# RWKV-7 chunk products of one core as 64x64 tiles on the four quadrants of TensorE, both scan directions side by side

## The chip, the cores and the metric

The kernel runs on one core of one Trainium2 chip. The metric is device microseconds from start to end of one execution, the median of the runs shown. TensorE (PE) does the matrix products, VectorE (DVE), ScalarE (ACT) and GpSimd (POOL) the element-wise work, and SyncE (SP) issues the DMAs.

## What is computed

Two layers of a bidirectional encoder (width 1024) on 2048 and 512 tokens. Layer 0 joins two gated linear recurrences. Layer 1 joins banded-window attention and RWKV-7 time mixing; the change is in the latter. Per head (8 heads of 64) and per direction it is this recurrence, and the two directions are added:

```python
def rwkv7_scan(r, log_w, k, v, kk, a):
    """S_t = S_{t-1} (diag(w_t) - kk_t (kk_t*a_t)^T) + v_t k_t^T, o_t = S_t r_t."""
    ...
    def step(S, inp):
        r_t, w_t, k_t, v_t, kk_t, b_t = inp
        s_kk = jnp.einsum('bhvk,bhk->bhv', S, kk_t)
        S = S * w_t[:, :, None, :] - s_kk[..., None] * b_t[:, :, None, :] + v_t[..., None] * k_t[:, :, None, :]
        return S, jnp.einsum('bhvk,bhk->bhv', S, r_t)
```

## The kernel before

Five stages follow each other: layer 0 with its input projection, its output projection, `layer1_proj` (projection of layer 1 and the element-wise preparation of the RWKV rows), `layer1_core` (attention and the RWKV recurrence) and the output projection of layer 1. All matrix products of `layer1_core` but the attention scores are plain float32; each such product is two records on TensorE (two weight loads, two passes), a transposition is one.

`layer1_core` works in 20 steps: 4 pairs of heads `p` times 5 blocks of 512 tokens. A step has two directions `d`, each two halves `hf` of four chunks `c` of 64 tokens. The two heads of a pair lie on partitions 0 to 63 and 64 to 127. Work is written as generators in lanes that take turns, and a planner of the framework then orders each engine's instructions at build time, by a simulated timeline and by priorities: `chain` first (1000), then `inverse` (600), then `stageT` (300), then `stageA` and attention.

- `stageA(n)` (lines 1279 to 1345) loads the prepared rows and makes, for each direction and half: `gram` (per head, 4 products 128x128x128 with a `KR` tile in which the other head's half is zero), its copy `GS`, masks into `LA`, `LD`, `OF`, `GB`, four transpositions `bk`, eight products `rps`, copied to `R`. PSUM: `pg`, two buffers of one bank.
- `inverse(n)` (lines 1347 to 1365): the 16x16 diagonal blocks of both directions go through DRAM (`lm`), are inverted by 28 small DVE operations and return through DRAM (`tm`).
- `stageT(n, d)` (lines 1367 to 1437), one lane per direction: reads `TC`, builds the 64x64 inverse in `TL` by 32x32 products `px`, `py`, `px`, `py`, then for each half `t1` (4 products), copies to `SW`, `fin` (2 times 4 products), sums into `RX`, copy to `OH`. PSUM: `pT`, two buffers of one bank.
- `chain(n, d)` (lines 1446 to 1492), one lane per direction, is the recurrence: per chunk a product `S0 x RX` (both heads at once), two DVE sums into `SS`, a transposition of `SS` on TensorE, an ACT copy scaled by the chunk's decay `ecol` to the next `S0`.
- `attention` (line 1561 on) runs beside: one block of 512 tokens of one group of heads for every two steps; per tile of 128 queries 4 score products, 12 transpositions `pt`, 3 products `po`. PSUM: `pa`, two buffers.

`stageA` of a step may be written at most NS = 4 halves ahead of `stageT`, since `GB`, `R` and `SW` have four buffers.

Of the kernel before, what the change touches and what calls it, by code (L numbers as in the profile page):

```python
# [40 lines left out]
class Common:  # L41
    def __init__(self, ctx, tc, a, seqs):
# [10 lines left out]
        self.lanes = {}  # L53
        nc.scalar.preload_act_table_set("natural_log_exp_and_others")
# [34 lines left out]
    def psums(self, ctx, l):  # L89
        f = lambda n, b: ctx.enter_context(self.tc.tile_pool(name=n + l, bufs=b, space=PSUM, reuse_waits="tile"))  # L90
        self.pp, self.pt, self.po = f("pp", 3), f("pt", 3), f("po", 2)

# [13 lines left out]
    def psum(self, n=NB):  # L106
        return self.pt.tile([128, n], F32, tag="t", name="pt")
# [711 lines left out]
def odd_cols():  # L819
# [7 lines left out]
    sw = list(range(64, 128)) + list(range(0, 64))  # L827
    for p in range(4):
        for off, perm in ((0, None), (512, None), (1024, sw), (1632, sw)):
            o = base + off + 128 * p  # L830
            out += [o + j for j in (perm or range(128))]
# [12 lines left out]
class Odd(Even):  # L844
# [47 lines left out]
    def rwkv_consts(self):  # L892
# [20 lines left out]
        self.xsc = self.const.tile([128, 2], F32, name="xsc")  # L913
        nc.vector.memset(self.xsc, 1.0)
        nc.vector.memset(self.xsc[0:64, 0:1], -0.5)
        nc.vector.memset(self.xsc[64:128, 1:2], -0.5)

        halves = slice(0, 64), slice(64, 128)
        self.bones = self.const.tile([128, 128], F32R, name="bones")
        self.swones = self.const.tile([128, 128], F32R, name="swones")  # L920
        for i in range(2):
            for j in range(2):
                q = halves[i], halves[j]
                self.act(self.bones[q], self.ident[q], AF.Copy, bias=float(i == j), scale=0.0)
                self.act(self.swones[q], self.ident[q], AF.Copy, bias=float(i != j), scale=0.0)
# [4 lines left out]
        self.v_scr = self.dram.tile([4, 2, nb, 64, 8, 128], F32, name="v_scr")  # L930
# [166 lines left out]
    def rwkv_rows(self, p, b, z):  # L1097
        nc, a = self.nc, self.a
        c64 = lambda t: t.rearrange("p (c t) -> p c t", t=RC)
        H0, H1 = slice(0, 64), slice(64, 128)  # L1100
# [68 lines left out]
        self.mm2(ps, self.swones, t)  # L1169
# [15 lines left out]
    def rwkv_dirs(self, p, b, kk, r, v, X1, X2, G):  # L1185
# [3 lines left out]
        for d in range(2):  # L1189
# [16 lines left out]
            self.stt(Z[:, 1, :, 0:64], view(X1), self.xsc[:, 0:1], e2, ALU.mult, ALU.mult)  # L1206
            self.stt(Z[:, 1, :, 64:128], view(X2), self.xsc[:, 1:2], e2, ALU.mult, ALU.mult)
# [13 lines left out]
    def layer1_core(self):  # L1221
        tc, nc, a = self.tc, self.nc, self.a
        with ExitStack() as ctx:
# [5 lines left out]
            pg, pT, pc = mkp("pg", 2), mkp("pT", 2), mkp("pc", 1)  # L1229
            pr = pg  # L1230
            self.pa = mkp("pa", 2)
            self.pt = pr
            mk = cp.tile([128, 2, 64], F32, name="mk")
            nc.sync.dma_start(out=mk, in_=a["mk"])
            mS = mk[:, 0:1].to_broadcast([128, 4, 64])
            mI = mk[:, 1:2].to_broadcast([128, 4, 64])
# [3 lines left out]
            M0, M1, MO = (mb[:, i:i + 1].to_broadcast([128, 8, 16]) for i in range(3))  # L1240
            ME = [mb[:, 3:4, i:i + 1].to_broadcast([128, 8, 16]) for i in range(2)]
# [10 lines left out]
            TL = [zeroed(f"TL{d}", [128, 8, 128], nc.vector) for d in range(2)]  # L1252
            SS = [[zeroed(f"SS{d}{i}", [128, 128], nc.vector) for i in range(2)] for d in range(2)]
            SW = [[[cp.tile([128, 4, 128], F32, name=f"SW{d}{i}{h}") for h in range(2)] for i in range(NS)] for d in range(2)]
            for i in range(NS):
                for d in range(2):
                    for h in range(2):
                        (nc.vector, nc.gpsimd)[h].memset(SW[d][i][h][Q[1 - h], :, Q[h]], 0.0)

# [500 lines left out]
```

## Time and profile before

| | us |
|---|---|
| median of 3 runs | 4167.64 (4167.12 to 4181.9) |
| the profiled execution | 4167.95 |
| its span, first to last instruction | 4166.2 |
| mean granted TensorE clock | 0.942 |

Over the span PE is busy 90%, DVE 68%, ACT 52%, POOL 27%. A busy PE is not a full PE: a record counts as busy until its result has left the array, so what the array really does is read from the distance between the starts of neighbouring records. `layer1_core` runs from about 2644 to 3808 us.

### The profile page before, as it was taken

The numbers are of one execution on the slowest core, as the hardware profiler recorded it, in microseconds if no ns is written. First come the engines' busy times: TensorE is split into PE (matmuls) and PEld (weight loads), VectorE is DVE, ScalarE is ACT, GpSimd is POOL, SyncE is SP. The second block draws the span as 40 slices with busy tenths as digits, with TensorE's granted clock in tenths as the row PEclk, the third lists the DMA queues.
The fourth block names the chain that finished last, engine by engine and source line by source line (L and its number), as shares of the span: only waits on it lengthen the run. The fifth ranks groups of instructions, "written<-read, shape, count | busy, mean of one in ns | idle before, by whom it ended". The sixth has DMA issues, their size and how long they took to land. (4 is left out here: it accounts for less than half of the span.)

```text
span 4166.2 us, 75101 instructions
## 1 busy us (share of the span) xinstructions
PE 3743.6 (90%) x27864; PEld 3067.3 (74%) x27864; DVE 2838.6 (68%) x6393; ACT 2149.8 (52%) x4198; POOL 1145.3 (27%) x1403
## 2 busy tenths in 40 slices
PE   6999999999888699999999989799999999995688
PEld 4878787777666577777777768578888888874567
DVE  4554545456666669757675768778777778775898
ACT  4565656555455432245454545556566666664220
POOL 1021212112211244423333322312222211113784
PEclk8999999999999799999999999899999999996889
DMA  7644445456555388768778876744454444534665
GB/s 264 215 144 165 167 148 202 155 193 217 210 207 198 109 251 253 232 230 263 242 258 260 252 250 218 197 103 117 109 121 116 118 119 118 125 79 150 222 223 173
DMA packets 768781, 770.20 MB, mean 185 GB/s; under 512 B 341632, under 2 KB 635136, under 8 KB 742816
## 3 DMA queue, kind: packets, MB, share of 16 engines
q1 hardware_dynamic: 768416, 765.40, 57.9%
q8 instruction: 221, 3.62, 0.4%
q14 instruction: 144, 1.18, 0.1%
HBM read 535.55 MB, written 220.20 MB: 181 GB/s over the span
## 5 line engine op out<-in xcount | busy, mean ns | idle before, releaser
L126 PE MATMUL pp<-h,whi 128*128 128x512 f32 (+2 forms) x4800 | 1565.7, 405 | 82.0 <-DMA h<-h_scr 29.0
L126 PEld LDWEIGHTS pp<-h,whi 128*128 128x128 f32 (+2 forms) x4800 | 895.4, 191 | 294.3 <-DMA h<-h_scr 30.5
L126 PE MATMUL pp<-h,wlo 128*128 128x512 f32 (+2 forms) x2400 | 958.5, 400 | 4.8 <-POOL wlo L113 4.7
L126 PEld LDWEIGHTS pp<-h,wlo 128*128 128x128 f32 (+2 forms) x2400 | 456.0, 190 | 110.5 <-POOL wlo L113 7.3
L110 ACT ACT_TABLE_LOAD x227 | 291.2, 1283 | 23.1 <-DVE cl L500 10.4
L126 PE MATMUL pp<-owh,oh 128*128 128x512 f32 x640 | 259.8, 406 | 23.6 <-DMA oh<-o_scr 22.6
L126 PE MATMUL pp<-owh,ol 128*128 128x512 f32 x640 | 256.2, 402 | 9.8 <-DMA ol<-o_scr 9.8
L1319 POOL COPY LD<-GS 32x128 f32<-32x128 f32 x320 | 115.1, 360 | 524.0 <-ACT GS L1316 508.7
L126 PE MATMUL pp<-owl,oh 128*128 128x512 f32 x640 | 259.1, 405 | 0.0
L113 POOL TENSOR_TENSOR wlo<-wst,whi 128x512 fp32r<-128x512 f32 (+3 forms) x87 | 161.0, 1856 | 248.4 <-ACT whi L110 244.8
L113 POOL TENSOR_TENSOR at<-abuf,abuf 64x256 f32<-64x256 f32 x80 | 63.7, 796 | 517.9 <-DVE abuf L530 448.3
L126 PE MATMUL gram<-KR,Zc 128*128 128x128 f32 x1280 | 188.5, 287 | 5.5 <-DMA KR<-z_scr 2.5
L126 PE MATMUL fin<-GB,SW 128*128 128x128 f32 x1280 | 179.4, 282 | 11.0 <-ACT OH L1433 8.1
L113 POOL TENSOR_TENSOR tmp<-tmp 128x512 fp32r<-128x512 f32 x80 | 116.6, 1457 | 256.6 <-ACT tmp L110 209.4
L113 DVE TENSOR_TENSOR SS<-chain,OH 64x64 f32<-64x64 f32 x608 | 135.1, 222 | 70.8 <-PE chain L126 59.5
L126 PEld LDWEIGHTS gram<-KR,Zc 128*128 128x128 f32 x1280 | 170.6, 201 | 8.6 <-ACT R L1334 3.1
L126 PEld LDWEIGHTS fin<-GB,SW 128*128 128x128 f32 x1280 | 161.2, 195 | 16.4 <-ACT OH L1433 11.4
L113 POOL TENSOR_TENSOR ptmp<-ptmp 128x512 f32<-128x512 f32 (+1 forms) x100 | 141.8, 1430 | 82.5 <-ACT ptmp L110 26.5
L126 PEld LDWEIGHTS pp<-owh,oh 128*128 128x128 f32 x640 | 125.5, 196 | 52.6 <-DMA oh<-o_scr 21.7
L110 ACT ACTIVATE S<-chain,ecol 128x128 f32<-128x128 f32 x320 | 115.4, 367 | 89.4 <-PE chain L141 86.0
L126 PEld LDWEIGHTS pp<-owh,ol 128*128 128x128 f32 x640 | 124.7, 195 | 37.7 <-DMA ol<-o_scr 11.7
L126 PE MATMUL chain<-RX,S 128*128 128x128 f32 x608 | 134.6, 310 | 14.0 <-DVE od L113 7.8
(327 smaller groups left out, 8330.5 us busy)
## 6 DMA issues: line engine op xcount, KB each, us to landing
h<-h_scr SPq DMA_DIRECT2D x70, 2048.0 KB, 9.2
h<-h_scr SPq DMA_DIRECT2D x80, 1024.0 KB, 7.4
z_scr<-Z SPq DMA_DIRECT2D x40, 1024.0 KB, 4.8
h_scr<-h SPq DMA_DIRECT2D x10, 2048.0 KB, 7.6
oh<-o_scr SPq DMA_DIRECT2D x40, 512.0 KB, 5.6
ol<-o_scr SPq DMA_DIRECT2D x40, 512.0 KB, 6.6
h_scr<-h1s SPq DMA_DIRECT2D x20, 1024.0 KB, 5.4
Zc<-z_scr SPq DMA_DIRECT2D x80, 256.0 KB, 3.2
```

The costliest lines, as they stand in the source:

```text
L110: self.nc.scalar.activation(out=out, in_=in_, func=func, bias=bias, scale=scale)
L113: (eng or self.nc.vector).tensor_tensor(out=out, in0=a, in1=b, op=op)
L126: self.nc.tensor.matmul(out=out, lhsT=lhsT, rhs=rhs, start=start, stop=stop)
L1319: nc.gpsimd.tensor_copy(LD[blk, cs], gs[blk, :, 32 * i:32 * i + 32])
```

## The change

In `layer1_proj` the two heads keep one order, so that three pairs of half-height DVE operations per block become three full ones, and `v_scr` is written by four DMAs per block and direction, not two. The columns and vectors that were swapped for this are no longer swapped.

In `layer1_core` the padding with zeros goes. Every chunk product becomes a 64x64 tile of the array: for direction 0 head h is read on its half and written on the same half, for direction 1 on the other half, so that the list `quads` names the four quadrants, and both directions share one tile (direction d in bank d of a PSUM tile of two banks). `stageA` and `stageT` run once per step for both directions; `pg` and `pT` become one buffer of two banks. `gram` becomes `gramb` and `gramk`; `bk` becomes products with diag(`ecol`) (made by POOL), so that `RX` carries the decay; `rps` becomes `kt` and `av`; `fin` becomes `finx` and `fino`, the latter with four 64-column products per chunk and quadrant. `t1` is read and written on the same half, so on two of the four quadrants. `chain` then needs per chunk two state products (one per head), one DVE sum and two output products: no transposition, no ACT copy. DMA loads per step fall from 32 to 12. `stageT` has one lane and single buffers (`TC`, `TE`, `TT`, `XS`, `T1`). In attention the lane yields after all four scores, and after every second transposed head.

The diff, cut to its core (what is removed stands in the code above):

```diff
@@ rwkv_rows @@
-        self.tt(X2[H0], k[H0], t[H0], ALU.mult)
-        self.tt(X1[H1], k[H1], t[H1], ALU.mult)
+        self.tt(X2, k, t, ALU.mult)
...
-        for h, x in ((H0, X2), (H1, X1)):
-            self.stt(t[h], r[h], self.rv[h, 5, p:p + 1], x[h], ALU.mult, ALU.mult)
-        self.stt(X1[H0], av[H0], 1.0, kk[H0], ALU.add, ALU.mult)
-        self.stt(X2[H1], av[H1], 1.0, kk[H1], ALU.add, ALU.mult)
+        self.stt(t, r, self.rv[:, 5, p:p + 1], X2, ALU.mult, ALU.mult)
+        self.stt(X1, av, 1.0, kk, ALU.add, ALU.mult)
@@ rwkv_dirs @@
-                nc.sync.dma_start(out=self.v_scr[p, d, db, :, o::2], in_=v4[64 * o:64 * o + 64])
+                for h in range(2):
+                    g = 64 * (h ^ d)
+                    nc.sync.dma_start(out=self.v_scr[p, d, db, g:g + 64, o::2],
+                                      in_=v4[64 * o:64 * o + 64, :, 64 * h:64 * h + 64])
@@ layer1_core @@
-            pg, pT, pc = mkp("pg", 2), mkp("pT", 2), mkp("pc", 1)
+            pg, pT, pc = mkp("pg", 1), mkp("pT", 1), mkp("pc", 1)
...
+            quads = [(d, Q[h], Q[h ^ d]) for d in range(2) for h in range(2)]
@@ stageA (new body of the loop over hf) @@
+                    kr = lp.tile([128, 2, 4, 192], F32, tag="KR", bufs=NS, name="KR")
+                    GB = lp.tile([128, 2, 4, 320], F32, tag="GB", bufs=4, name="GB")
...
+                    for d in range(2):
+                        nc.sync.dma_start(out=Z[:, d], in_=self.z_scr[p, d, b, :, 1, cs])
+                        nc.sync.dma_start(out=kr[:, d, :, 0:128], in_=self.z_scr[p, d, b, :, 0, cs])
+                        nc.sync.dma_start(out=vs[:, d], in_=self.v_scr[p, d, b, :, cs])
+                    gc = 8 * b + 4 * hf
+                    self.tt(kr[:, :, :, 128:192], iib,
+                            self.ecol[:, p, :, gc:gc + 4].unsqueeze(3).to_broadcast([128, 2, 4, 64]), ALU.mult, nc.gpsimd)
+                    two = lambda name: pg.tile([128, 2, 4, 128], F32, tag="t", name=name)
+                    gb = two("gramb")
+                    for c in range(4):
+                        for d, q, o in quads:
+                            self.mm(gb[o, d, c], Z[q, d, c, 0:64], kr[q, d, c, 0:128])
+                    gs = lp.tile([128, 2, 4, 64], F32, tag="GS", bufs=2, name="GS")
+                    nc.scalar.copy(gs, gb[:, :, :, 0:64])
+                    self.tt(GB[:, :, :, 192:256], gb[:, :, :, 64:128], mI, ALU.mult)
...
+                    gk = two("gramk")
+                    for c in range(4):
+                        for d, q, o in quads:
+                            self.mm(gk[o, d, c], Z[q, d, c, 64:128], kr[q, d, c, 0:128])
+                    self.tt(GB[:, :, :, 0:128], gk, mSI, ALU.mult)
+                    yield
+                    bk = two("bk")
+                    for c in range(4):
+                        for a in range(2):
+                            for d, q, o in quads:
+                                self.mm(bk[o, d, c, 64 * (1 - a):64 * (2 - a)], Z[q, d, c, 64 * a:64 * a + 64],
+                                        kr[q, d, c, 128:192])
+                    for d in range(2):
+                        nc.scalar.copy(GB[:, d, :, 64:320].rearrange("p c (a t) -> p c a t", t=128)[:, :, :, 64:128],
+                                       bk[:, d].rearrange("p c (a t) -> p c a t", t=64))
+                    yield
+                    kt = two("kt")
...
+                            self.mm(kt[o, d, c, 0:64], kr[q, d, c, 0:64], II[q])
+                    nc.scalar.copy(R[:, :, :, 0:64], kt[:, :, :, 0:64])
+                    yield
+                    av = pg.tile([128, 2, 4, 64], F32, tag="t", name="av")
...
+                            self.mm(av[o, d, c], GB[o, d, c, 0:64], vs[o, d, c])
+                    nc.scalar.copy(R[:, :, :, 64:128], av)
...
+                self.tt(L1, LD[:, :, 16:32], M1, ALU.mult, nc.gpsimd)
...
@@ stageT @@
-            def stageT(n, d):
+            def stageT(n):
...
+                prod = lambda name: pT.tile([128, 16, 32], F32, tag="t", name=name)
...
+                    t1 = two("t1")
                     for c in range(4):
+                        for d in range(2):
+                            for q in Q:
+                                self.mm(t1[q, d, c], TL[q, 8 * d + 4 * hf + c], R[q, d, c])
+                    T1 = lp.tile([128, 2, 4, 128], F32, tag="T1", bufs=1, name="T1")
+                    nc.scalar.copy(T1, t1)
                     yield
...
+                    f = two("finx")
+                    for c in range(4):
+                        for d, q, o in quads:
+                            self.mm(f[q, d, c], T1[o, d, c, 0:64], GB[o, d, c, 192:320])
+                    self.tt(RX, f, kr[:, :, :, 64:192], ALU.add)
+                    yield
+                    f = two("fino")
+                    for c in range(4):
+                        for d, q, o in quads:
+                            self.mm(f[q, d, c, 0:64], T1[o, d, c, 64:128], GB[o, d, c, 192:256], start=True, stop=False)
...
+                    nc.scalar.copy(OH, f)
@@ chain @@
+                        for q in Q:
+                            self.mm(po[q, 4 + c], RX[q, c, 64:128], S0[d][q])
+                        self.tt(s0, po[:, 4 + c], OH[:, c, 64:128], ALU.add)
+                        for q in Q:
+                            self.mm(po[q, c], S0[d][q], RX[q, c, 0:64])
                         S0[d] = s0
                         yield
+                    self.tt(o4[:, 4 * hf + i:4 * hf + 4], po[:, i:4], OH[:, i:4, 0:64], ALU.add)
```

## Rows read from the trace of the kernel before

**Rows 1.** busy time by stretch: PE, PEld, DVE, ACT, POOL, granted clock, DMA, GB/s

```profile
1860.00:2644.00 784.00, 713.58 (x3085) 569.26 (x3083) 562.88 (x752) 396.95 (x653) 243.09 (x289) 0.96 0.76 251
2800.00:3700.00 900.00, 854.00 (x11691) 756.33 (x11690) 700.17 (x2598) 569.08 (x1441) 182.50 (x484) 0.96 0.49 119
3700.00:3808.00 108.00, 90.01 (x1066) 68.75 (x1065) 75.33 (x256) 63.04 (x149) 29.18 (x33) 0.88 0.27 81
```

**Rows 2.** tiles `gram` and `acc_scr`: ns min/median/max, first and last start

```profile
L126 PE MATMUL gram<-KR,Zc x1280: 270/275/582, 2644.7 to 3705.4; 128*128 128x128 f32 x183
...
L1487 SPq DMA_DIRECT2D acc_scr<-od x40: 319/335/1579, 2787.7 to 3807.8; - x40
```

**Rows 3.** order of time on PE: start, us together, records

```profile
3000.44 1.05 PE L126 MATMUL gram<-KR,Zc 128*128 128x128 f32 x8
3007.63 0.39 PE L126 MATMUL rps<-II,KR 128*128 128x64 f32 x2
3012.42 2.74 PE L126 MATMUL po<-pT,vw 128*128 128x512 f32 x6
3018.16 0.59 PE L126 MATMUL score<-kw,q 128*128 128x384 f32 x2
```

**Rows 4.** groups on PE from 2800 to 3700: busy us, mean ns, idle before

```profile
L126 PE MATMUL gram<-KR,Zc 128*128 128x128 f32 x1042 | 152.9, 285 | 1.0 <-ACT GB L1327 0.4 <-ACT R L1334 0.3
L126 PE MATMUL po<-pT,vw 128*128 128x512 f32 x168 | 80.7, 610 | 0.0
L126 PE MATMUL score<-kw,q 128*128 128x384 f32 x194 | 62.0, 413 | 0.1
L141 PE MATMUL pt<-c_ident,pr 128*128 128x128 f32 x336 | 54.1, 283 | 0.4 <-DVE pr L121 0.4
```

**Rows 5.** order of time on PE, smaller tiles of layer 0

```profile
333.19 0.22 PE L126 MATMUL pb<-qb,k 128*64 128x64 f32 x1
333.24 0.22 PE L126 MATMUL pb<-qb,k 128*64 128x64 f32 x1
...
1246.22 0.28 PE L126 MATMUL pa<-qb,k 64*64 64x128 f32 x2
1246.43 0.28 PE L126 MATMUL pa<-qb,k 64*64 64x128 f32 x2
```

**Rows 6.** order of time on PE where 128x128 and 32x32 tiles alternate

```profile
3033.07 0.27 PE L141 MATMUL chain<-c_ident,SS 128*128 128x128 f32 x1
3033.28 0.31 PE L126 MATMUL px<-TT,LO 32*32 32x32 f32 x12
3033.52 0.33 PE L141 MATMUL chain<-c_ident,SS 128*128 128x128 f32 x1
3033.78 0.65 PE L126 MATMUL px<-TT,LO 32*32 32x32 f32 x52
```

**Rows 7.** order of time on ACT: first copy and last copy of one `stageT`

```profile
3087.59 0.37 ACT L1385 COPY XS<-px 128x256 f32<-128x256 f32 x1 [0.78 <-PE px L126]
...
3137.00 0.58 ACT L1433 COPY OH<-fin 64x512 f32<-64x512 f32 x1
```

**Rows 8.** groups on DVE, ACT and POOL: busy us, mean ns, idle before

```profile
L113 DVE TENSOR_TENSOR SS<-chain,OH 64x64 f32<-64x64 f32 x499 | 110.9, 222 | 53.2 <-PE chain L126 44.0
L113 DVE TENSOR_TENSOR RX<-fin,rho 64x256 f32<-64x256 f32 x132 | 54.9, 416 | 3.7 <-PE fin L126 1.7
...
L113 DVE TENSOR_TENSOR kk<-kk,tmp 128x512 f32<-128x512 f32 x18 | 12.4, 691 | 13.6 <-ACT tmp L110 13.4
...
L110 ACT ACTIVATE S<-chain,ecol 128x128 f32<-128x128 f32 x262 | 94.8, 367 | 65.9 <-PE chain L141 63.2
L1316 ACT COPY GS<-gram 128x512 f32<-128x512 f32 x130 | 75.2, 582 | 20.8 <-PE gram L126 17.9 <-PE chain L141 2.0
...
L113 POOL TENSOR_TENSOR Z<-mr,e 128x512 f32<-128x512 f32 x40 | 56.5, 1413 | 149.6 <-ACT e L110 95.7 <-DMA z_scr<-Z 40.5 <-issue 13.3
```

**Rows 9.** the issues of `v_scr` on SP: ns min/median/max

```profile
L1217 SPq DMA_DIRECT2D v_scr<-tmp x80: 508/567/1965, 1844.8 to 2629.9; - x80
```

More of the change, by code (lines that the diff above doesn't have):

```diff
@@ L826, in odd_cols @@
     base = 1280
-    sw = list(range(64, 128)) + list(range(0, 64))
     for p in range(4):
-        for off, perm in ((0, None), (512, None), (1024, sw), (1632, sw)):
-            o = base + off + 128 * p
-            out += [o + j for j in (perm or range(128))]
+        for off in (0, 512, 1024, 1632):
+            out += list(range(base + off + 128 * p, base + off + 128 * p + 128))
     out += list(range(base + 1536, base + 1632))
@@ L929, in rwkv_consts @@
         self.z_scr = self.dram.tile([4, 2, nb, 128, 2, 8, 128], F32, name="z_scr")
[L930 removed]
+        self.v_scr = self.dram.tile([4, 2, nb, 128, 8, 64], F32, name="v_scr")
         self.g_scr = self.dram.tile([4, nb, 128, NB], F32, name="g_scr")
@@ L1251, in zeroed @@
                 return t
[L1252 to L1258, printed above, removed]
-            KR = [zeroed(f"KR{i}", [128, 4, 2, 2, 64], nc.gpsimd) for i in range(2)]
-            la = zeroed("LA", [128, 4, 128], nc.vector)
+            TL = zeroed("TL", [128, 16, 64], nc.vector)
             II = cp.tile([128, 64], F32, name="II")
@@ L1386, in stageT @@
                 yield
-                y = pT.tile([128, 8, 32], F32, tag="t", name="py")
-                for c in range(8):
+                y = prod("py")
+                for c in range(16):
                     for g in range(4):
@@ L1392, in stageT @@
                 self.tt(te, te, y, ALU.add)
+                nc.vector.transpose(out=tt, in_=te)
                 for i in range(2):
-                    nc.vector.transpose(out=tt[B1[i]], in_=te[B1[i]])
-                    nc.scalar.copy(tl[B2[i], :, B2[i]], te[B2[i]])
-                    nc.gpsimd.tensor_copy(tl[B1[i], :, B1[i]], te[B1[i]])
+                    nc.scalar.copy(TL[B2[i], :, 32:64], te[B2[i]])
+                    nc.gpsimd.tensor_copy(TL[B1[i], :, 0:32], te[B1[i]])
                 yield
-                x = pT.tile([128, 8, 32], F32, tag="t", name="px")
-                for c in range(8):
+                x = prod("px")
+                for c in range(16):
                     for i in range(2):
@@ L1406, in stageT @@
                 yield
-                y = pT.tile([128, 8, 32], F32, tag="t", name="py")
-                for c in range(8):
+                y = prod("py")
+                for c in range(16):
                     for i in range(2):
                         self.mm(y[B1[i], c], xs[B2[i], c], te[B2[i], c])
-                nc.scalar.copy(tl[B1[0], :, B2[0]], y[B1[0]])
-                nc.vector.tensor_copy(tl[B1[1], :, B2[1]], y[B1[1]])
+                nc.scalar.copy(TL[B1[0], :, 32:64], y[B1[0]])
@@ L1439, in layer1_core @@
+                    nc.scalar.copy(OH, f)
+                    for d in range(2):
+                        rx[n, d, hf] = (RX[:, d], OH[:, d])
+                    nT[0] += 1
+                    yield
             rx = {}
             S0 = [None, None]
-            ns = [0, 0]
             acc = set()
@@ L1733, in prep @@
     r["sin"] = f(np.concatenate([-sn, sn, -sn, sn], 0).astype(np.float32))
-    wo = g["od_w_out"][0].copy()
-    rows = np.arange(1024)
-    for p in range(4):
-        o = 512 + 128 * p
-        rows[o:o + 128] = o + sw
-    r["wout1"] = f(wo[rows])
     return r
```

218 lines of the change are left out of this document (78 added, 140 removed).

## Prediction

> **What bounds the kernel now.** I read first the busy times by stretch. The change touches `layer1_proj` and `layer1_core`. In the former PE is busy 713.6 of 784 us, in the steady part of the latter 854 of 900, with DVE at 700, ACT at 569, POOL at 183 and DMA at 0.49 [rows 1]. Then the length of a step: the first `gram` starts at 2644.7, and the 40 stores of `acc_scr` (two per step) run from 2787.7 to 3807.8 [rows 2], so the first step needs 143 us to pass through all lanes, and each of the 19 others adds 53.7 us.
>
> Then, how full PE is. Eight `gram` records take 1.05 us together and one alone 0.27, so they start 0.111 us apart; two `rps` records take 0.39, which is again 0.11 apart, though they have only 64 columns [rows 3, 6]. Weights of 128 columns set this pace, not the streamed ones. `po` starts every 0.43 us, `score` every 0.18 [rows 3, 4], `px` every 0.009: (0.65 - 0.31)/40 [rows 6]. Per step, each float32 product being two records: `gram` 64, `fin` 64, `rps` 64, `t1` 32, `bk` 16 and `chain` 46 (30 products, 16 transpositions) are 286 x 0.111 = 31.8 us; `px` and `py` 384 x 0.009 = 3.5. Attention: 900 us hold 1042/64 = 16.3 steps, and 168 x 0.43 + 194 x 0.18 + 336 x 0.111 = 144 us [rows 4], 8.8 per step (the few shorter scores left out). A change of tile costs as well: a 32x32 record starts 0.21 after a 128x128 one that it follows, not 0.11 [rows 6], so 0.1 each; eight `px` or `py` groups per step, each cut once by `chain`, make 32 changes, 3.2 us. Sum 47.3 of 53.7: PE is 88% full, and 6.4 us are waits. So PE's work sets the pace, the more since it takes its queue in order.
>
> **The change, products.** Do smaller tiles run side by side? In layer 0, where four 64x64 tiles on all four quadrants (two with 128 streamed columns, two with 64) make one chunk, a chunk's first passes start at 1246.22 and the next chunk's at 1246.43 [rows 5]. Four calls of two passes each thus take 0.21, no more than two passes of one call. For 64 columns, two passes on a 64-column tile start 0.05 apart (333.19, 333.24), 0.11 per call [rows 5]. So I price a set of four calls at 0.22 with 128 columns and at 0.11 with 64. Not shown are four tiles all 128 wide or all 64 wide; if they overlapped only as far as those rows prove (three quarters of the columns), a set of 128 would take up to 0.29, and one of 64 up to 0.15.
>
> Per half: `gramb`, `gramk`, `finx` 12 sets of 128 = 2.64; `t1`, on two quadrants only, 8 x 0.22 = 1.76; `bk` 8, `kt` 4, `av` 4, `fino` 16 sets of 64 = 3.52. Both halves: 15.8 us. They replace 240 records, 26.6 us: **-10.8**. `chain`: 15.2 chunks x 2 pairs x 0.11 = 3.3 for 5.1: **-1.8**. `px` and `py` keep their 384 records.
>
> **Tile changes.** Attention stays at 128x128 and so becomes a stranger among 64x64 tiles. A step holds two query tiles of nine groups each (4 `score`, 4 `pt`, 1 `po`): 36 changes if each group stands alone (3.6 us), 4 if each query tile stays together (0.4). Attention fills gaps at the lowest priority, so I take **+3.4**.
>
> PE after: 47.3 - 10.8 - 1.8 + 3.4 = 38.1. The waits I leave at 6.4: step 44.5, that is -9.2.
>
> **Other engines.** DVE: 32 `SS` sums of 0.22 become 15; 16 `RX` sums of 0.42 become two of 1024 elements, between 0.69 and 1.38 each (512 elements: 0.69), taken at 1.2: together -7.9 of some 43 us. ACT loses 16 scaled copies of 0.37; 8 `GS` copies of 0.58 become two; what is doubled in length (`T1`, `OH`) takes between 0.58 and 1.16, taken at 1.0 [rows 8]. Both engines get lighter and neither is the bound, so this is priced at nothing; were DVE the bound, it would be worth those 7.9. POOL gets a 512-element product per half for diag(`ecol`), 1.41 us by its nearest row [rows 8], ahead of `bk` only, with `gramb`, `gramk` and their copies as cover; uncovered 2.8 per step. DMA loads fall from 32 to 12 per step: nothing, as loads run ahead.
>
> **Added waits.** `pg` and `pT` now have one buffer: `gramk` cannot start before `GS` and the masked product have left `gramb`, and so at each of five places per half; in `stageT` eight to ten times per step. What stands behind such a product in PE's queue (attention, `chain`, the other stage) waits too, unless the planner put other work between. From below this costs nothing (the 6.4 even shrink, since `chain` hands over twice per chunk, not four times); from above it is the second rival. I take zero net.
>
> **`layer1_proj`.** Three DVE operations fewer per block, at most 0.69 each [rows 8], are 41 us of DVE, but PE does 91% there: nothing. 80 more `v_scr` issues of 0.57 us [rows 9] stand in SP's queue ahead of loads; these are made a block early, so nothing; uncovered, up to 46 us.
>
> **Sum.** First step: its eight chunks shrink from 0.38 + 0.44 + 0.27 + 0.37 to 0.38 + 0.22, -7 us. 19 x -9.2 - 7 = -182: from the 4167.95 of the profiled execution (span 4166.2 and 1.75 around it; the median is 0.3 less) **3986 us**.
>
> **Rivals.**
> 1. *Waits shrink too.* Tile changes stay at 3.2 (PE 34.7) and waits fall in proportion, to 4.7: step 39.4, -14.3, 3889 us. For it: every engine is lighter, and the recurrence has half the hand-overs. Against it: one buffer where two were.
> 2. *`stageT` sets the pace.* It becomes one lane, serial through one buffer: `px` 1.2, copy 0.6, `py` 1.2, sum 0.7, transposition 0.7, `px` 0.6, copy 0.7, `py` 0.6, copy 0.7, then twice `t1` 1.8, copy 1.0, `finx` 0.9, `RX` 1.2, `fino` 1.8, copy 1.0: 22 us, and some 20 hand-overs of 0.15 (a record's 0.27 less 0.11): 25 us. The same count before, with the pieces at half size and two lanes in two buffers, is 18 us, and one `stageT` took 3087.59 to 3137.58, 50 us [rows 7], 2.8 times as much, because each hand-over waits in full queues. At a stretch of 2 the step is 50: -77, 4091 us. The Trainium skill warns of this ("TensorEngine Tiling (Array Packing)", "PSUM Bottleneck"): after the speed-up the copies out of PSUM may bind. The rows agree as to the place, but the copies get fewer.
> 3. *Slower:* the same lane keeps its stretch of 2.8: 70 us per step, +16.3 x 19 - 7 = +303, 4471 us. It decides from a stretch of 53.7/25 = 2.15 on. Against it: the stretch comes from PE's fullness, which falls.
> 4. *The quadrants don't overlap:* 128 calls of 0.22 and 256 of 0.11 per step are 56.3 us, not 15.8; step 85, +31.3 x 19 - 7 = +588, 4756 us. The two passes between 1246.22 and 1246.43 [rows 5] speak against it.
> 5. *Narrow sets are no cheaper than wide ones,* because records can't start closer than the eight records in 0.21 us that the quadrants have shown, 0.026 each [rows 5]. Then a set of 64 costs 0.22: +3.52 x 2 + 3.3 = +10.3, step 54.8, +14, 4182 us: no change. Against it: `px` records start 0.009 apart [rows 6]. Such a floor, of about 25 ns, is stated by the Trainium skill ("TensorE: Matmul & The Clock Gate", section "Wait — 56ns, not 53.3ns?"); as an estimate from that figure, the 768 + 122 + 384 records of a step would take 31.9 us.
>
> Inside the forecast lies the clock: at the 0.88 of a stretch with less work, not 0.96 [rows 1], PE's 38.1 grow by 3.5, +66 us.
>
> **How the numbers follow.** Forecast 0.57 (own range 3930 to 4060), rival 1 0.17, rival 2 0.14, rival 3 0.07, rival 4 0.02, rival 5 0.03. The range 3880 to 4110 leaves out the deep end of rival 1 (under its 3889), the late end of rival 2, and rivals 3 to 5, together about 0.2; the dearer sets (32 x 0.04 + 12 x 0.07 per half, +4.2 per step, 4066) lie in it. A measurement of this kernel tells 0.5% from no change. Slower by more: rivals 3 and 4, 0.09; within: rival 5 and the tail of rival 2, 0.05; faster by more: 0.86.
>
> **What the changed profile would show.** Right: `gramb` sets 0.22 apart, `fino` sets 0.11, the step 42 to 48 us, PE still the fullest engine, `chain` between its products with one DVE sum. Wrong if: sets take twice that; PE waits long for ACT or DVE ahead of `gramk`, `finx` or `fino` (rival 2); from `XS` to the last `OH` copy of a step 53 us or more (rival 3); many more tile changes than 70 per step; a granted clock under 0.88 in `layer1_core`.

## The result, and the profile after

The changed kernel takes 4374.57 us (median of 4 runs, 4373.28 to 4378.36), the kernel before beside it 4171.38: ratio 1.0485, 95% interval 1.0462 to 1.0507. It is slower by 4.9%, where 3986 us were forecast. The profiled execution has a span of 4373.4 us against 4166.2, and a mean granted clock of 0.901 against 0.942.

First the busy times by stretch (columns as in [rows 1], here PE, PEld, DVE, ACT, POOL, granted clock, DMA, GB/s): the projection, the first step, and from the first to the last store of `acc_scr`.

```profile
1860.00:2656.40 796.40, 702.67 (x3019) 559.49 (x3018) 493.05 (x641) 386.01 (x618) 240.79 (x283) 0.95 0.73 240
2656.40:2766.50 110.10, 80.68 (x1835) 64.59 (x1836) 49.55 (x166) 34.79 (x82) 18.54 (x37) 0.73 0.38 109
2766.50:4037.00 1270.50, 966.24 (x24652) 767.69 (x24650) 589.96 (x1802) 418.59 (x883) 234.72 (x402) 0.82 0.30 84
```

The same view of the kernel before, between its first and last store:

```profile
2787.70:3807.80 1020.10, 955.36 (x12834) 834.80 (x12834) 787.17 (x2895) 638.81 (x1603) 214.19 (x524) 0.96 0.46 115
```

And the tiles that mark the steps in the changed kernel (to be read against [rows 2]):

```profile
L128 PE MATMUL gramb<-KR,Zc x1280: 267/269/473, 2656.4 to 3950.6; 64*64 64x128 f32 x183
...
L1489 SPq DMA_DIRECT2D acc_scr<-od x40: 319/377/1659, 2766.5 to 4037.0; - x40
```

The 207.2 us are: the core starts 11.7 later, its first step is 110.1 instead of 143.0 (-32.9), the 19 others take 1270.5 instead of 1020.1 (+250.4), and what follows the last store 336.4 instead of 358.4 (-22.0). So a step went from 53.7 to 66.9 us, while every engine got emptier. PE is busy 50.9 us of a step (966.24 / 19), before 50.3; idle 16.0, before 3.4. That PE's busy time did not fall, though its work did, is the clock: busy time times granted clock, an estimate of its work at the full clock, is 41.7 us a step against 48.3. At the old clock of 0.96 that work would be 43.4 us busy. So a step changed, by this estimate, by -6.9 (less work), +7.5 (clock) and +12.6 (idle).

The two steps are not quite like for like, since stageA of the kernel before runs further ahead and is through sooner: of the 20 steps of `gram` 16.7 lie in its window (1068 of 1280 records), of the 20 of `gramb` 18.0 (1152 of 1280). So part of the -32.9 and of the +250.4 is the same work, moved from the first step into the window. Up to the store by which stageA ends (16 steps of the kernel before, 18 of the changed one) every step is full (PE alone, first before, then after):

```profile
2787.70:3671.70 884.00, 839.89 (x11462) 0.97 0.49 119
```

```profile
2766.50:3964.20 1197.70, 923.96 (x23689) 0.83 0.30 82
```

A full step went from 55.3 to 66.5 us, idle from 2.8 to 15.2, and the same estimate gives -8.6 (less work), +7.4 (clock) and +12.4 (idle). The account stays; the difference of a step is 11 us and not 13.

**One stall, on three engines.** PE in order of time (start, us together, records, and in brackets how long PE was idle before and what ended it):

```profile
3063.88 1.02 PE L143 MATMUL pt<-c_ident,pr 128*128 128x128 f32 x6
3075.75 1.11 PE L128 MATMUL bk<-KR,Zc 64*64 64x64 f32 x26 [10.85 <-DVE GB L115]
...
3086.08 0.49 PE L128 MATMUL px<-TT,LO 32*32 32x32 f32 x18 [3.91 <-DVE S L115]
...
3108.04 1.10 PE L128 MATMUL gramk<-KR,Zc 64*64 64x128 f32 x32
```

DVE in the same time:

```profile
3066.35 0.43 DVE L115 TENSOR_TENSOR LC<-LC,L 128x256 f32<-128x256 f32 x1
3071.80 0.18 DVE L115 TENSOR_TENSOR tp<-A 128x14 f32<-128x14 f32 x1 [5.02 <-DMA A<-lm]
...
3074.48 1.22 DVE L115 TENSOR_TENSOR GB<-gramk,mk 128x1024 f32<-128x1024 f32 x1
...
3084.49 0.69 DVE L115 TENSOR_TENSOR TE<-TC,mkb 128x512 f32<-128x512 f32 x1 [4.74 <-DMA TC<-tm]
```

`bk` waits for the one PSUM tile `pg`, which DVE empties with the product of `gramk` into `GB`; that product stands in DVE's queue behind the first half of the inverse, and the inverse behind its trip through DRAM. `px` and `chain` then wait behind the second trip. PE's clock over this stretch, in windows (PE busy, clock, DMA, GB/s):

```profile
3040.00:3064.00 24.00, 22.85 (x669) 1.00 0.34 99
3064.00:3076.00 12.00, 1.15 (x14) 0.66 0.27 62
3076.00:3104.00 28.00, 23.38 (x490) 0.72 0.18 49
3104.00:3124.00 20.00, 15.69 (x512) 1.00 0.33 100
```

While PE is 95% busy it has the upper level, 2.4 GHz; after the idle stretch much of the next 28 us is at the lower, 1.2 GHz, although PE works again. The Trainium skill describes this ("TensorE: Matmul & The Clock Gate", section "HAM oscillation — how this bites in real kernels"): a matmul loop that waits longer for DMA than it computes pays for the wait and then starts each burst slow. The rows agree, though what PE waits for directly is DVE, which waits for the DMA.

PE's groups between the first and the last store (busy us, mean ns, idle before and what ended it):

```profile
L128 PE MATMUL po<-pT,vw 128*128 128x512 f32 x208 | 129.0, 759 | 0.4
...
L128 PE MATMUL chain<-RX,S 64*64 64x64 f32 x1104 | 89.5, 271 | 73.0 <-DVE S L115 63.8 <-DVE A L1364 8.7
...
L128 PE MATMUL bk<-KR,Zc 64*64 64x64 f32 x2304 | 80.8, 267 | 92.1 <-DVE GB L115 91.3 <-issue 0.5
...
L128 PE MATMUL px<-TT,LO 32*32 32x32 f32 x2304 | 34.6, 221 | 40.5 <-DVE TT L1381 20.3 <-DVE S L115 20.1
```

Two thirds of PE's 304 us of idle time stand before `bk`, `chain` and `px`, and DVE ends nearly all of it. `po`, which the change doesn't touch, takes 759 ns a record where it took 610 [rows 4]. DVE's own waits for the two trips (us, times, longest):

```profile
DVE tp L115 <- DMA A<-lm: 84.5, 18, 5.9
...
DVE TE L115 <- DMA TC<-tm: 76.9, 18, 5.8
```

In the kernel before these are 24.8 and 22.5 us.

### The profile page after: what moved, and what is told of

It is laid out like the page before. It is cut to its first block, busy times and chain, and to the rows that moved or that the text cites. A ratio compares the mean times of both kernels' runs of the same rounds, so it can differ in the third digit from the quotient of the medians.

```text
span 4373.4 us, 95466 instructions
## 1 busy us (share of the span) xinstructions
PE 3701.0 (85%) x39928; PEld 2944.2 (67%) x39928; DVE 2525.5 (58%) x5020; ACT 1878.4 (43%) x3334; POOL 1142.1 (26%) x1213
## 4 chain that ended last, share of the span: by engine, by line
PE 25%; DVE 12%; DMA 8%; issue 3%; ACT 3%; POOL 2%; SPq 1%; POOLq 0%; DVEq 0%; ACTq 0%
PE pp L128 10%; PE po L128 2%; DMA lm<-LC 2%; DMA h<-h_scr 2%; PE t L128 1%; PE fino L128 1%; PE av L128 1%; DVE tp L115 1%; DMA TC<-tm 1%; PE py L128 1%; PE chain L128 1%; DVE A L115 1%; DVE pr L123 1%; PE px L128 1%; POOL ptmp L115 1%
## 5 line engine op out<-in xcount | busy, mean ns | idle before, releaser
L112 ACT ACT_TABLE_LOAD x227 | 291.2, 1283 | 22.9 <-DVE cl L502 12.4
L128 PE MATMUL pp<-owh,oh 128*128 128x512 f32 x640 | 258.1, 406 | 12.4 <-ACT owh L112 6.2
L128 PE MATMUL bk<-KR,Zc 64*64 64x64 f32 x2560 | 88.9, 269 | 95.5 <-DVE GB L115 94.8
L128 PE MATMUL chain<-RX,S 64*64 64x64 f32 x1152 | 93.2, 271 | 75.0 <-DVE S L115 65.8
L128 PEld LDWEIGHTS pp<-owl,oh 128*128 128x128 f32 x640 | 125.5, 196 | 33.0 <-DVE owl L115 5.6
L128 PEld LDWEIGHTS bk<-KR,Zc 64*64 64x64 f32 x2560 | 74.0, 172 | 106.5 <-DVE GB L115 98.7
L115 POOL TENSOR_TENSOR tmp<-tmp,yh 128x512 fp32r<-128x512 f32 x40 | 56.4, 1411 | 311.5 <-ACT yh L112 223.3
L128 PE MATMUL po<-pT,vw 128*128 128x512 f32 x224 | 136.7, 748 | 0.4
L128 PEld LDWEIGHTS chain<-RX,S 64*64 64x64 f32 x1152 | 72.1, 167 | 94.1 <-DVE S L115 80.3
L1617 ACT ACTIVATE pr<-pr,nm 128x384 f32<-128x384 f32 (+1 forms) x160 | 94.6, 591 | 88.6 <-DVE nm L1615 88.0
```

What stands on the lines that cost most here:

```text
L112: self.nc.scalar.activation(out=out, in_=in_, func=func, bias=bias, scale=scale)
L115: (eng or self.nc.vector).tensor_tensor(out=out, in0=a, in1=b, op=op)
L128: self.nc.tensor.matmul(out=out, lhsT=lhsT, rhs=rhs, start=start, stop=stop)
L1617: nc.scalar.activation(out=pr[:, 0:nk], in_=pr[:, 0:nk], func=AF.Exp, bias=nm[:, hd:hd + 1], scale=-1.0, accum_out=den[:, hd:hd + 1])
```

## The experiments

Five groups, each built on what was open after the one ahead. In the table all but the ratio is from the view of busy times between the first and last `acc_scr` store, over 19 steps (in the last two rows, in the part without attention: 10 and 4 full steps); tile changes are neighbouring PE records of different tile size, counted over the same window. `a_` is the changed kernel with an edit, `b_` the kernel before. The ratio is to the kernel before.

| run | ratio (95% interval) | step us | PE busy | PE idle | clock | tile changes per step |
|---|---|---|---|---|---|---|
| before | 1 | 53.7 | 50.3 | 3.4 | 0.96 | 27 |
| after | 1.0485 (1.0462 to 1.0507) | 66.9 | 50.9 | 16.0 | 0.82 | 39 |
| a_direct | 1.0281 (1.0238 to 1.0323) | 63.1 | 52.2 | 10.8 | 0.83 | 48 |
| b_direct | 0.9845 (0.9809 to 0.9881) | 52.2 | 49.8 | 2.4 | 0.97 | 26 |
| a_gk_act | 1.0554 (1.0517 to 1.0591) | 68.6 | 51.3 | 17.2 | 0.81 | 43 |
| a_bufs2 | 1.0457 (1.0416 to 1.0497) | 66.7 | 50.6 | 16.0 | 0.82 | 39 |
| a_one | 1.0786 (1.0762 to 1.0810) | 73.4 | 59.3 | 14.1 | 0.76 | 65 |
| a_pg2 | 1.0837 (1.0818 to 1.0855) | 73.8 | 60.5 | 13.3 | 0.77 | 76 |
| a_pT2 | 1.0643 (1.0624 to 1.0662) | 69.6 | 56.6 | 13.0 | 0.79 | 57 |
| a_av | 1.0627 (1.0611 to 1.0643) | 68.7 | 54.3 | 14.5 | 0.80 | 52 |
| a_lead | 1.0544 (1.0509 to 1.0580) | 67.1 | 51.5 | 15.6 | 0.80 | 40 |
| a_lcfirst | 1.1381 (1.1347 to 1.1414) | 84.1 | 70.7 | 13.4 | 0.71 | 99 |
| b_ns2 | 0.9972 (0.9953 to 0.9991) | 54.4 | 50.6 | 3.8 | 0.96 | 31 |
| a_priA | 1.0590 (1.0553 to 1.0627) | 67.0 | 49.9 | 17.1 | 0.83 | 26 |
| a_prog | 1.0958 (1.0929 to 1.0988) | 72.9 | 50.9 | 22.0 | 0.79 | 20 |
| a_progd | 1.1339 (1.1322 to 1.1356) | 79.3 | 53.5 | 25.8 | 0.75 | 20 |
| a_nosim | 1.1147 (1.1127 to 1.1167) | 64.3 | 52.2 | 12.1 | 0.83 | 39 |
| b_nosim | 1.0905 (1.0885 to 1.0924) | 59.7 | 55.3 | 4.4 | 0.93 | 18 |
| a_attfirst | 1.0681 (1.0638 to 1.0725) | 62.0 | 39.3 | 22.7 | 0.74 | 12 |
| b_attfirst | 0.9979 (0.9964 to 0.9993) | 47.5 | 43.5 | 4.0 | 0.99 | 28 |

### 1. The round trips

```diff
# a_direct; b_direct does the same with its two halves of LC
-                LC = lp.tile([128, 16, 16], F32, tag="LC", bufs=1, name="LC")
+                LC = self.wk.tile([128, 16, 16], F32, tag="A", bufs=2, name="A")
...
-                nc.sync.dma_start(out=A, in_=lms[n % 2].rearrange("d c (g s) t -> (d c g) s t", s=16))
+                A = data[n, "A"]
...
-                nc.sync.dma_start(out=TC, in_=tms[n % 2].rearrange("d c p t -> p (d c) t"))
+                TC = data.pop((n, "A"))
```

> The changed kernel with the two round trips of the inverse through DRAM shortened to nothing: the inverse works in the tile LC itself and stageT reads that tile as TC; both writes to lm and tm are still issued, the two loads A and TC are left out (the block layout is then another, so the numbers that come out are others; all instructions of DVE, PE and ACT are the same). Theory trip (DVE's queue stands in two DRAM round trips of each step, the 1024-wide product of gramk, the chain's sums and the transposition behind them come late, PE goes idle and its clock falls): the waits tp on A and TE on TC, 84.5 and 76.9 us over 19 steps, go, with part of PE's waits for DVE behind them and part of the clock: 4040 to 4210 us, PE idle a step from 16 to below 9 us, clock above 0.87. Theory one buffer (A's only PSUM tile makes gramk, its product and bk take turns): the turns stay, 4310 to 4374. Theory small tiles (64x64 tiles are granted a lower clock whatever waits there are): clock stays at 0.80 to 0.85 in the core, 4200 to 4374.

> The kernel before with the same cut: the inverse works in a tile that both directions' LC are written to, stageT reads its halves, the loads A and TC are left out. Theory trip: the kernel before has the same two round trips, but its waits for them are 24.8 and 22.5 us over 19 steps and PE has other work meanwhile (idle 3.4 us a step): 4110 to 4171 us. If before gains as much as the changed kernel (160 us or more), the round trips are no difference between the two, and theory trip falls.

The changed kernel gained 2.0% of the time before, the kernel before 1.6%. PE's idle time fell by 5.2 us a step, but only 3.8 of them reached the step: PE's busy time grew by 1.3 at the same clock. So the trips are 3.8 us of a step of the changed kernel against 1.5 of the kernel before, 2.3 of the 13.2 lost. Theory trip had the mechanism, but two to four times its size, and neither its idle time (below 9) nor its clock (above 0.87) came. The range of theory small tiles held the time and the clock, but the windows above show 64x64 tiles at 1.00. The cut was not complete: the inverse now works in the tile that the store to `lm` still reads, and waits for that (waits of a_direct):

```profile
DVE A L115 <- DMA lm<-A: 42.3, 18, 4.8
```

### 2. Buffers

```diff
# a_gk_act
-                    self.tt(GB[:, :, :, 0:128], gk, mSI, ALU.mult)
+                    nc.scalar.copy(GB[:, :, :, 0:128], gk)
+                    self.tt(GB[:, :, :, 0:128], GB[:, :, :, 0:128], mSI, ALU.mult, nc.gpsimd)
# a_bufs2: LD, LC, TC, TE, TT, XS, T1
-  bufs=1
+  bufs=2
# a_one, a_pg2, a_pT2, a_av: both chains in one bank
-                    po = pc.tile([128, 8, 64], F32, tag=f"c{d}", name="chain")
+            PC = pc.tile([128, 2, 4, 64], F32, tag="c", name="chain")
# buffers of pg, pT, pa: a_one 1, 1, 1; a_pg2 2, 1, 1; a_pT2 1, 2, 1; a_av 1, 1, 2 and one bank for av
```

> The changed kernel with gramk taken out of PSUM by an ACT copy, its mask multiplied on POOL in SBUF, instead of the one product on DVE; the rest as it was. Theory one buffer: bk's wait for DVE's product (91.3 us over 19 steps, 4.8 a step) goes almost whole, and the clock gains: 4200 to 4300. Theory trip: the wait goes here as well, since ACT has no round trip in its queue, but the chain's sums and the T stage still stand behind the trips: 4250 to 4340. Theory single SBUF tiles (TE, TT, XS, T1, TC, LD hold the stages back): no gain, 4350 to 4400.

> The changed kernel with two buffers where the change left one: LD, LC, TC, TE, TT, XS and T1 (L1 keeps one). Theory single SBUF tiles: the stages of successive steps overlap again, 4150 to 4300. Theories trip and one buffer: PE's waits are for DVE's queue and for PSUM, nothing changes but the planner's order, 4330 to 4400.

> The control for the two: chain of both directions in one bank, one bank instead of two for attention, pg and pT with one buffer as in the changed kernel; two banks are left unused. All theories: the changed kernel's 4374 plus 0 to 50 us for attention, which now takes turns with itself: 4370 to 4425.

> The changed kernel with two buffers of two banks for pg, the products of stageA. The room: the chain of both directions in one bank (kept tile, sums of the outputs two chunks at a time) and one bank less for attention, both as in a_one. Theory lane A (stageA is one lane with one PSUM tile; its five products a half start one after the other, 6.39, 4.78, 7.37, 8.82 and 6.21 us apart in the profile of the changed kernel, 67 us a step, which is the step): the turns overlap, the step falls from 66.9 to 50 to 58 until stageT's 41 us and its wait for the inverse bind, idle falls below 10 us a step: 4130 to 4260 us, and at least 100 under a_one. Theory T (stageT's one tile pT): within 40 us of a_one. Theory order (what holds PE is the place of DVE's work in its queue, whatever buffers there are): within 60 us of a_one.

> The same room given to pT instead: two buffers of two banks for stageT's products, one for stageA's. Theory lane A: stageT is through in 41 of the step's 67 us and then waits, so nothing is gained: within 50 us of a_one, 4340 to 4420. Theory T: at least 100 us under a_one. Theory order: within 60 us of a_one.

> The changed kernel with the chain in one bank as in a_one, attention with its two banks, and the bank that is freed given to av, the last of stageA's five products: pg has one buffer and four products a half to serve. Theory lane A: the turn of av (6.2 us a half, less what the turns of the others grow) goes out of the row, the step falls by 6 to 12 us: 4150 to 4270. Theory T: 4350 to 4390. Theory order: 4320 to 4400.

All these expectations of a gain failed, and a_one's too: its bound of 50 us was 4425, it took 4492. What held were the rival expectations of no gain: 4330 to 4400 in a_bufs2, and theory order's 60 us around a_one in a_pg2 (+23) and a_pT2 (-52); a_gk_act (4419) and a_av (4430) came out above all their ranges. Two buffers in SBUF changed nothing. In a_gk_act the wait before `bk` went, as wanted, and PE then waited before `chain` (PE's groups of a_gk_act):

```profile
L128 PE MATMUL chain<-RX,S 64*64 64x64 f32 x1107 | 90.8, 275 | 172.8 <-DVE S L115 158.8 <-DVE A L1365 12.1 <-issue 1.8
L128 PE MATMUL bk<-KR,Zc 64*64 64x64 f32 x2304 | 86.8, 263 | 2.2 <-issue 1.8 <-ACT GB L1312 0.4
```

92.1 us fell to 2.2, 73.0 rose to 172.8. The same with two buffers of `pg` (PE's groups of a_pg2; in a_one `bk` waited 44.2, the two `chain` groups 77.7 and 33.3):

```profile
L128 PE MATMUL chain<-RX,S 64*64 64x64 f32 x1104 | 119.9, 283 | 101.6 <-DVE S L115 100.7
L128 PE MATMUL chain<-S,RX 64*64 64x64 f32 x1104 | 112.1, 275 | 69.0 <-DVE od L115 58.2 <-DVE RX L115 10.5
L128 PE MATMUL bk<-KR,Zc 64*64 64x64 f32 x2240 | 99.2, 255 | 0.5 <-issue 0.4
```

In both, a wait that was taken away in PE's queue turned up at another instruction that needs DVE; idle time stays at 13 to 17 us. The last four runs are not clean, since they pay for the shared bank: `chain` waits there for the sums `od` too, which it does not in the changed kernel, and tile changes rise from 39 to between 52 and 76. Against a_one, a second buffer for `pT` gives 1.4%, one for `pg` costs 0.5%.

### 3. How far stageA runs ahead

From the last `fino` of a step to the first `px` of the next the changed kernel needs 22.7 us on the mean (18 gaps between the records): `LC` of the next step comes only then. Three ways to bring it forward, and the reverse in the kernel before:

```diff
# a_lead
+            for n in range(2):
+                self.add("A", stageA(n))
+            self.drain("A")
# a_lcfirst: in stageA, LC with its store and LO moved up, behind gramb of both halves
# a_priA
-                self.add("A", stageA(n))
+                self.add("A", self.urgent(stageA(n), 800))
# b_ns2
-            NS = 4
+            NS = 2
```

> The changed kernel with stageA written out for two steps before the first stageT, instead of for one (its limit of four halves ahead stands); nothing else. Theory lead: in the changed kernel LC of a step comes at the end of the stageT of the step before, so inverse and both round trips stand between one stageT and the next (22.7 us from the last fino to px on the mean), where the kernel before has them beside stageT; with A a step further ahead that gap goes below 10 us, and the step falls by 8 to 15: 4090 to 4220 us. Theory own pace (each of A's ten products a step waits 6.7 us for its turn whatever stands beside it): A can't keep the lead, which is used up in the first steps: 4330 to 4380. Theory order: 4300 to 4400.

> The changed kernel with stageA's products in another order: gramb of both halves, then LC, its store and LO, then gramk, bk, kt and av of both halves; the same instructions. Theory lead: the inverse of the next step can start after two of A's ten products instead of seven, some 30 us earlier, beside stageT: gap before px below 10 us, 4090 to 4220. Theory own pace: the inverse comes earlier, but the ten turns still take 67 us: gap smaller, step within 3 us of 66.9, 4310 to 4380. Theory order: 4300 to 4400.

> The changed kernel with stageA issued at a priority of 800, above the inverse (600) and stageT (300), below the chain (1000); before it had none. Theory lead: A runs up to its limit of four halves ahead, the gap before px falls below 12 us: 4130 to 4280. Theory own pace: A's products come out of the queue sooner, each turn falls from 6.7 to about 5 us: 4150 to 4300, with the gap as it was or larger. Theory order (attention and stageT lose what A gains): 4330 to 4450.

> The kernel before with stageA at most two halves ahead of stageT instead of four (NS 2, which also halves the buffers SW). Theory lead: it gets the changed kernel's sickness: inverse and round trips come between one stageT and the next, idle rises from 3.4 to above 9 us a step and the clock in the core falls from 0.96 to below 0.91: 4300 to 4500. Theory small tiles (64x64 tiles lower the clock by themselves): the time may rise, the clock stays at 0.94 or more. Theory own pace: two lanes with two buffers make up for the shorter lead: 4170 to 4250.

Only two of the four test theory lead. What stageA has made when the first `px` of a step starts (counted in `gram` or `gramb` records) is the step's own products and no more in the changed kernel, and the same in 17 of 20 steps of a_lead, which left the gap at 19.7 us; in the kernel before it is three quarters of the next step as well, and b_ns2 left that as it was in most steps. So b_ns2, 0.3% faster than the kernel before, says nothing of a shorter lead. a_priA, a whole step ahead, closed the gap to 3.1 us and a_lcfirst to 7.4, and neither got faster: with these theory lead fell. Theory order's range held a_lead (4386) and a_priA (4408); a_lcfirst (4736) lay above all three. In a_priA other waits came instead (PE's waits of a_priA):

```profile
PE chain L128 <- DVE S L115: 73.2, 55, 5.1
PE gramb L128 <- DMA KR<-z_scr: 55.9, 46, 4.0
```

a_lcfirst shows where the gap goes (its PE in order of time):

```profile
3094.62 0.31 PE L128 MATMUL px<-TT,LO 32*32 32x32 f32 x2
3094.86 0.47 PE L128 MATMUL av<-vs,GB 64*64 64x64 f32 x2
3095.26 0.31 PE L128 MATMUL px<-TT,LO 32*32 32x32 f32 x2
```

The planner lays the records of `px` and `av` alternately, two by two, between the steps of `chain`: 0.64 us for four records (at a clock of 0.50 here), where an uncut `px` of 128 records takes 1.4 us in a_prog (3007.5 to 3008.9, at 1.00). The first `px` of a step is spread over 18.4 us on the mean (over 14.9 in a_priA, over 2.5 in the changed kernel), with 99 tile changes per step and a clock of 0.71.

### 4. The planner's order

```diff
# a_prog (a_progd: also DVE's tensor_tensor), within the core
+            self.tc.keep_in_program_order(ins)
# a_nosim, b_nosim
-    with tile.TileContext(nc, schedule_with_timeline_sim=True) as tc:
+    with tile.TileContext(nc, schedule_with_timeline_sim=False) as tc:
```

> The changed kernel with PE's instructions in the core kept in the order in which the lanes write them (one product of stageT, one chunk of each chain, one product of stageA, one piece of attention, in turn), not in the planner's; the other engines as planned. Theory order (the planner's order on PE is the loss: products are cut up and laid between the chain's hand-overs, where PE then stands still): no product is cut, idle falls below 10 us a step, the clock rises above 0.87, 4050 to 4280 us. Theory structure (the merged stages wait for each other in any order): idle stays at 14 to 20 us a step, 4340 to 4500.

> As a_prog, and DVE's products and sums in the core in the written order as well, so that the product of gramk no longer stands behind the inverse's round trip unless it is written so. Theory order: as a_prog or up to 100 us better, 4000 to 4280. Theory structure: 4340 to 4550.

> The changed kernel with the planner's simulated timeline turned off for the whole program (it then orders by a simpler rule); layer 0 and the projections get another order too, so the step in the core is compared, 66.9 us with the timeline. Theory order: the step falls or rises less than in b_nosim, and comes within 8 us of b_nosim's. Theory structure: it stays 10 us or more above b_nosim's.

> The kernel before with the same timeline turned off; 53.7 us a step with it. Both theories: the timeline knows this kernel's 128x128 products well, so the step rises by 3 to 15 us.

With PE's order taken from the program the products are whole (20 tile changes), yet PE stands still for 22.0 us a step, mostly before `chain` (waits of a_prog):

```profile
PE chain L134 <- DVE S L115: 311.9, 291, 5.9
```

That is as theory structure said, and worse; with DVE pinned as well (a_progd) it is 25.8 us. The pair without the timeline speaks for the other side (busy times by stretch, PE alone; first a_nosim, then b_nosim):

```profile
3073.70:4296.00 1222.30, 992.55 (x24818) 0.83 0.32 88
```

```profile
3023.50:4158.60 1135.10, 1051.15 (x13521) 0.93 0.43 109
```

The changed kernel's core gained 2.6 us a step and the other lost 6.0, with PE busy 5.0 us longer; the difference shrank from 13.2 to 4.6 us, as theory order said. So the size of the difference depends on the order that this planner finds for each of the two kernels. That another order would win most of the loss back for the changed one is not shown: its own gain is 2.6 us, and it still idles 12.1 us a step, the other 4.4.

### 5. Attention moved away

```diff
# a_attfirst, b_attfirst
+            self.stepA = 99
             self.add("X", self.attention())
+            self.drain("X")
```

> The changed kernel with the whole attention written ahead of the core instead of beside it. The total grows by what attention takes alone; to be read is the step in the part of the core that is free of attention (66.9 us with it, PE idle 16.0). Theory structure (the lanes' dependences set the pace, attention only fills waits): the step stays at 56 to 67 us, idle rises to 20 us or more. Theory order (attention's pieces, their tile changes and their share of DVE's and ACT's queues delay the hand-overs): the step falls by more than the 10.7 us of PE that attention takes, to 40 to 54 us, idle below 14.

> The kernel before with attention ahead of the core in the same way. Its step of 53.7 us holds 9.3 us of attention on PE and 3.4 of idle. Both theories: PE's work sets its pace, so the step falls by about what attention took, to 42 to 48 us, idle 3 to 7. If it stays above 50, the kernel before is held by its dependences as well.

The planner still lays attention beside the first steps (the last `score` starts at 3278.7 in a_attfirst, at 3461.3 in b_attfirst), so only what comes after is read, and in b_attfirst only as long as stageA runs (PE busy, clock, DMA, GB/s; a_attfirst over 10 steps, then b_attfirst over 4):

```profile
3426.90:4047.10 620.20, 393.42 (x12660) 0.74 0.23 64
```

```profile
3510.70:3700.80 190.10, 173.99 (x2754) 0.99 0.45 107
```

This is the clearest pair. Taking attention away shortens a full step before from 55.3 to 47.5 us, as it must where PE's work sets the pace, and in the changed kernel only from 66.5 to 62.0, while 12.0 us of busy time went and idle rose to 22.7. PE's work at full clock (busy times clock, an estimate) is 29.1 us a step here against 43.1: the quadrants do save 14 us. The step is 62.0 against 47.5 all the same. Theory structure was right on step and idle: PE is busy 63% of the time, its work at the full clock would fill 47%, and attention is not there to delay anything; the lanes of the changed core wait for each other. One such wait (a_attfirst, PE in order of time):

```profile
3553.88 2.08 PE L128 MATMUL gramb<-KR,Zc 64*64 64x128 f32 x32 [0.69 <-ACT R L1335]
3566.64 1.93 PE L128 MATMUL px<-TT,LO 32*32 32x32 f32 x128 [10.68 <-DVE TT L1381]
3568.50 0.92 PE L128 MATMUL gramk<-KR,Zc 64*64 64x128 f32 x12
```

and DVE in the same time:

```profile
3565.05 0.69 DVE L115 TENSOR_TENSOR TE<-TC,mkb 128x512 f32<-128x512 f32 x1 [4.60 <-DMA TC<-tm]
3565.78 0.71 DVE L1381 STREAM_TRANSPOSE TT<-TE 128x512 f32<-128x512 f32 x1
3566.41 0.65 DVE L115 TENSOR_TENSOR GB<-gramb,mk 128x512 f32<-128x512 f32 x1
```

The second trip of one step's inverse holds DVE, behind it stands the product that empties `pg` for `stageA` of the next step, and PE has only `px` and `gramk` to go on with, which need the one and the other: 10.68 us for nothing.

## Why the prediction was wrong, step by step

- **Prices of the sets: right.** 32 records of `gramk` (four sets) in 1.10 us, each lasting 0.27, start 0.027 apart, so a set of eight takes 0.21, where 0.22 was taken. `fino` at the full clock starts twelve sets, 96 records, in the 1.40 us between these two rows of PE in order of time: 0.0146 a record, 0.117 a set, where 0.11 was taken.

```profile
3117.72 0.32 PE L128 MATMUL fino<-GB,vs 64*64 64x64 f32 x6
...
3119.12 0.32 PE L128 MATMUL fino<-GB,vs 64*64 64x64 f32 x6
```

  Rivals 4 and 5 are out with this. The floor of about 25 ns between starts that the Trainium skill states ("TensorE: Matmul & The Clock Gate", section "Wait — 56ns, not 53.3ns?") doesn't hold here: the rows show 14.6 ns for tiles on the four quadrants.
- **PE's work: nearly right.** In full steps without attention it fell by 14 us, where 10.8 + 1.8 was forecast; with attention by 8 (50.9 to 42.6), where 9.2 was forecast, all by the estimate of busy time times clock. Tile changes rose by 12 a step (27 to 39), not by 34.
- **"The waits I leave at 6.4": the step that failed.** Of these the profile counts 3.4 as idle (a busy PE is not a full one), and that became 16.0: +12.6 us a step, 239 us in all. The reasoning took PE's fullness as the cause of the pace and the waits as a remainder that stays. That they had been short because another lane's products covered each hand-over, and that this cover went when the products got cheaper and both directions shared one lane, fits the pair without attention; no run separates the two, so as a cause it is argued. The 53.7 itself was read from a window with 16.7 steps of `gram`; against a full step of 55.3 the same sum leaves 8 us of waits.
- **The clock: noticed, mis-sized and kept out of the sum.** The variant at 0.88 was worth 66 us; it became 0.82 and cost 7.5 us a step, 142 us. In the windows above it falls in and after the idle stretch, so there it belonged to the waits and was no term of its own.
- **Added waits "at zero net": wrong.** The upper bound, rival 2, looked at `stageT` alone. But `stageT` got no slower: from its first `XS` to its last `OH` copy a step takes 44.6 us on the mean of 20, against 50 for one direction before [rows 7] and the 53 that rival 3 asked for. What came late was its start.
- **Rival 3** had the sign and about the size (4471 against 4375), and its mechanism, `stageT` setting the pace, is not what the trace shows. Rival 1 is out.
- **DVE, ACT at nothing: right** that they are no bound (31.1 and 22.0 us a step); but DVE's place in the order, not its load, now ends most of PE's waits.
- **First step:** -32.9, not -7. Of this some 21 us are stageA's work that moved out of it, an estimate: 1.3 steps of its 144 records, 0.111 each. **`layer1_proj`: not nothing.** DVE fell by 70 us, where 41 at most was forecast, yet the core starts 11.7 us later. PE's waits there for loads of `h` grew from 18.1 to 35.8 us; that they stand behind the added stores of `v_scr`, which the prediction put at up to 46 us uncovered, is the candidate, and this wasn't tried.
- Of the signs named as "wrong if", one appeared, the clock; PE's waits came ahead of `bk`, `chain` and `px`, not of `gramk`, `finx`, `fino`.

**What is shown, and what stays open.** Shown: the loss is idle time and a lower clock, not the price of the products; none of the buffers and single waits that were changed carries it (those in PSUM were tried only with the chains in one bank), and attention doesn't; the round trips are about 2.3 of the 13.2 us, and the difference depends on the planner's order (4.6 under another, though mostly because the kernel before lost by it). Open: which dependence sets the 62 us of the core without attention. The serial row of two trips, inverse and `stageT` is a candidate: in a_attfirst, from 3658 on, the time from the last `fino` of a step to the first `px` of the next is in turn 27.8, 1.2, 26.0, 1.2, 28.9, 1.2 and 23.8 us. But the trips were only half cut, a_priA closed that gap without a gain, and no run gives each direction its own lane again with the quadrants kept.

## What to carry to other kernels

When the change makes the fullest engine's work cheaper, ask what each wait was covered by, and work out the longest row of hand-overs of one step (product, copy, trip) as a second bound beside the engine's work. A wait at the head of a queue is only worth removing if the instruction behind it is ready too: compare the sum of idle time, not that one wait. Where two lanes are merged to halve the instructions, ask whether their waits merge too; here this is argued, not shown.

## What the runs showed of the hardware

PE's granted clock did not follow its idle time alone. In a_lcfirst PE counts as busy 84% of the time (1344.03 of 1598.70 us), much of it in pieces of two records with a tile change between, and the clock is 0.71, lower than in a_attfirst with PE 63% busy (0.74):

```profile
2751.80:4350.50 1598.70, 1344.03 (x24799) 0.71 0.23 66
```

So a busy share by itself says little of the clock. Why it was lower there stays open. The 64x64 tiles do not lower it by themselves: in the changed kernel they ran at 1.00 from 3040 to 3064 and from 3104 to 3124.

In that kernel, at the full clock, PE started 64x64 records of 64 columns on the four quadrants 14.6 ns apart and those of 128 columns 27 ns apart (the rows of `fino` and `gramk` above).
